# A delta-rule decoder layer: the key scale is made on VectorE in two operations, GpSimd's chains of a head lose two operations, and the order of all instructions is drawn up anew

## The chip, the cores and the metric

The kernel runs on one core of one Trainium2 chip. The time is the device time of one execution in microseconds (us); it is quoted as the median of three runs. The engines are TensorE (PE; its weight loads are shown apart as PEld), VectorE (DVE), ScalarE (ACT), GpSimd (POOL) and SyncE (SP), which here issues the loads and stores. Each engine works through its own instructions strictly in the order in which the program issues them, and waits on semaphores for results of the others.

## The reference

One decoder layer on 2048 tokens of width 1024 in float32: a gated delta-rule mixer with 8 heads of 128, a cross-attention with 4 heads on a memory of 256 rows, an output projection, a layer norm, and a squared-ReLU MLP of width 4096 with a second layer norm. The change lies in the mixer:

```python
qkv = silu(causal_depthwise_conv(qkv, conv_w))
q = l2_normalize(heads(q)); k = l2_normalize(heads(k)); v = heads(v)
beta = sigmoid(b);  g = -exp(a_log) * softplus(a + dt_bias)
# in chunks of 64 tokens, with gc = cumsum(g) and decay = exp(gc_i - gc_j):
lower  = strict_lower((k*beta) @ k.T * decay);   a_mat = I + lower
u      = solve(a_mat, v*beta);  w = solve(a_mat, k*beta*exp(gc))
v_new  = u - w @ state
o      = (q*exp(gc)) @ state + ((q @ k.T) * decay) @ v_new
o      = rms_norm(o, gate_norm_w) * silu(z)
```

`l2_normalize` divides by sqrt(sum of squares + 1e-6). The kernel leaves q and k as they come from the convolution and puts their norms into factors of one number a token. `bh` is such a factor: beta divided by the squared norm of k, which stands on the rows of `lower`.

## The kernel before

**Stages.** The tokens are four blocks of 512. Two blocks form a super. The program runs the mixers of blocks 0 and 1, the output projection of the first super, its first and second MLP product (`ff1`, `ff2`), a stage that prepares the gate `z` of blocks 2 and 3 (`gate_seven`), the mixers of blocks 2 and 3, and the output projection and MLP of the second super. Large products are made of float32 values split into a high and a low half, so that one product is three matmuls of 128x128 on 128x512 (`mm3`; in the profile `aq`, `ak`, `av`, `az` are the projections for q, k, v and the gate, and `fA`, `f2A` and the like belong to the MLP). Weights come by DMA as `wraw` or, split already, as `whl`; `T` is a token tile that was transposed and split, `xj` its raw form at the start.

**A mixer** is a pipeline over its 8 heads. In step t it issues `dense` for head t, `gdn_a` for head t-1 and `gdn_b` for head t-2.

- `dense` makes q, k and v (`aq`, `ak`, `av`, then the convolution in `raw`, `cq`, `ck`, `cv`), transposes k and q on TensorE (`ptk`, `ptq`), and ACT sums their squares into `ss` (four columns for k, four for q; its scratch outputs are `jk`, `jq`). From `ss` GpSimd makes `rk` (power -1/2 of k's part), `e4` (`e` in the profile; from q's part), `vbs`, `bh` and `nbe`.
- `gdn_a` loads a head's decay logarithms (`gb`), makes `dl` and `at` with them, multiplies k with k and q (`pkq`), scales `dl` by `bh` on VectorE, inverts the triangular matrix (`invert`: `inv`, `pp`, `pq`, `Z`, `ZT`, `X`, `Y`), and transposes v (`ptv`), which ACT scales by `vbs`.
- `gdn_b` runs through the chunks with the state (`pc`, `po`); ACT sums the squares of the output into `oss`, GpSimd makes `m4` (`m` in the profile) and `ro` (power -1/2), ACT scales the output (`on`), TensorE transposes it (`pto`) and VectorE multiplies it with the gate.

`gates` makes, once a block, the factors of all heads: `beta`, `betah`, `neg`, the decay sums `gc`.

**What sets the order.** Nothing is issued where it is written. A `Recorder` takes all operations down, and `issue` gives them to the engines in an order that is stored in the program as a table of numbers (`ORDER`); a second table (`SLOT`) says which buffer of its kind each tile gets. Both were made for this list of operations. All recorded instructions therefore have one line in the profile, L615 before and L673 after; groups must be told apart by tile names.

```python
out = [self.ops[i] for i in order()]
...
for o in out:
    o.fn(*[res(a) for a in o.args], **{k: res(v) for k, v in o.kw.items()})
```

Of the kernel before, what the change touches and what calls it, by code (L numbers as in the profile page):

```python
# [14 lines left out]
P = 128  # L15
TB = 512
NC = TB // P
D = 1024
# [153 lines left out]
class Op:  # L172
# [4 lines left out]
    "c-rlK+m7ryuH+A;0qZXP|BsF0LfKiX*6!U8Gr$0iK4-72s!XS?3q=Nl!TZxb>Fa;vbCplke-?gmt@c^{bEO+U<$J%%e5d|8Cx5v1b@rduep%Y*"  # L177
    "!aJ^V^H1ed@TXGwRr{}H?Q87+>_6ah<&!3Uv0voIPw|&{cdq+(a=Ue{JO8-X=YLo4_;0E|e!p<L<Nd4sZJ(O=9kd%S^<Uh7>YuqEbDja&pWAQR"
    "cT#bC`_lWVu6<AY&dR<3o}$e0X}DO$jaG~jK3+0!yZ!ZcfBoP7bX^}`sEz$^FH_g5ciq3iNbhfIpS&<jt#DrUsO|sZZu6dteaHJ!_x$7XIsMa@"
    "UpberH?QB`wx=uafxh<F;tp2V{Pr8aZ=ZVeRy&uBK2p~HOeuBG?7kv~td4sR`ox3mk?o&eu~MdQV?PDHq@1s;{B6O^x5NS37p+=eHG9P--tLuj"  # L180
    "Ke^(5_IKgMzZ?4tUw~<@`$p=(eBWGjTH<vt0o?k``(ZKUcxTxIzjs0z{8oIX@8w%+;q~?#unjPIX|Mjob(gq#_WKJ~(tgN_B~ub-vGjuFv+p0*"
    "%9VQ%tDx*R=C*%V2EI<$ANz^17we~#j<5bNR@xpn4*H%lJx=F7%+rsCUk*%a&HK%G!P{sWslj>OPrX-o|7gSIS-p(*_Q53P#oNE~p6!fbyZ?*("
    "%lfC|rmlf~x9==3OuxRNW6NRs_YCb7MC;<o-wSc>5nM7Y*WL&FUHELCdn@DF@eEwKyvKn#n_(fkmOZDf?U8Qdr$O0^40{qQq{E1815+?JFhP4M"
    "VyrMpSp$Wiw^`Z0ygwuRseGZSEv%ogx%b6z+dcO$!?quwr}A2=xW`UI$ysUp`b8EO6S4;&-dynYnHGERn~}I`GjEE6muSugE%08G`%(9}?JwNB"
    "b?s~JEAMsnwj}$>_8-#T`>FG)^W0GUuQdMZZTiaVX)5Om_J8gb-|zsHyL{jO{{E%QH7=KoJ=gbl?0;ZSVSccCN*y{)_$e&^sr9&$c3kF7U->a^"
    "iP!sjmZ=*}`W-9|J|H{TxDxiy+z^vz*tKoU9?AjpHtxoIyc*8|O!ofnhQ~>Jv3Cw+;v(Q7um==_pZV|;AK`OuL)fr}_WC(52A1~NciLdv+cu=V"
    "$N26gsar4FYI~aaV*O#v*RyQ%`rY1Rt)+Zcb^E0LPg`>6*shq&H8g)%@%yItVYQkp2Y=Xi$=CZP_@HnawhOTh3|DQD3D;V#T;XF6H+IUzD#bHi"
    "_-D26qu{sO%2|h3{$W7I_t_R(2S-RQG%y_-pjTL#vhS_6ire2u()Kd;A;wJ!!v!OeCYD--(b<czby^4PttLC4ZklK8js2U<cf-Vwh3j#}FJ8Fe"
# [443 lines left out]
def hybrid_layer(  # L632
# [46 lines left out]
    def small(name, shape, bufs=3, dt=F32):  # L679
        return rec.buf(sm, shape, dt, name, bufs, name)  # L680
# [1458 lines left out]
```

## Time and profile before

| | |
|---|---|
| runs | 2700.58, 2701.74, 2702.75 us (median 2701.74) |
| the profiled execution's own time | 2704.81 us |
| its span from first to last instruction | 2703.1 us |
| granted TensorE clock, mean | 0.998 of full speed |
| instructions in the profile | 42569 |
| bytes moved by DMA | 633.73 MB, 234 GB/s |

The stages lie in the span at about 0 to 20 us (start), 20 to 345 (mixer of block 0), 345 to 612 (block 1), 612 to 756 (output projection), 756 to 1373 (MLP), 1373 to 1410 (`gate_seven`), 1410 to 1690 (block 2), 1690 to 1965 (block 3), 1965 to 2100 (output projection) and 2100 to 2703 (MLP, last layer norm and store). A row of a group reads: line, engine, operation, output<-inputs, shapes, count, then busy us and mean ns of one, then the idle time of the engine just ahead of such instructions and what ended it. A row of waits reads: engine, what it was about to run, what it waited for, then us in total, how many, the longest.

### The profile page before, as it was taken

Reading aid. Unit: us, or ns where it says so; the run is one execution under the profiler, and the core shown is the slowest. Engines: PE = TensorE matmul, PEld = TensorE weight load, DVE = VectorE, ACT = ScalarE, POOL = GpSimd, SP = SyncE. Lnnn points to the kernel's source line nnn. Section 1 sums busy time; section 2 is a strip of 40 time slices with the busy share of each in tenths; the row PEclk is TensorE's granted clock in tenths of the full one; section 3 lists DMA queues with packets and bytes.
Section 4 is the critical chain, followed back from the end, with each engine's and each line's share of the span. In section 5 each row is a group of like instructions: output and inputs, shape, how many; then the busy total and the mean of one; then the engine's idle time right before and its main releaser. Section 6 shows DMA issues by size and latency. Waiting matters only on the chain.

```text
span 2703.1 us, 42569 instructions
## 1 busy us (share of the span) xinstructions
PE 2681.2 (99%) x13553; PEld 2248.4 (83%) x13553; DVE 2129.6 (79%) x5658; ACT 1643.1 (61%) x4128; POOL 426.5 (16%) x1023
## 2 busy tenths in 40 slices
PE   9999999999999999999999999999999999999998
PEld 7888888888888888878888888888888888888887
DVE  7999889998877776766787887999978656567475
ACT  7778767786575555333445777777756555544342
POOL 3233233331000000000012332332201000000011
PEclk9999999999999999999999999999999999999999
DMA  8767558877888888889785444545678654486673
GB/s 296 262 216 280 185 181 288 310 255 264 279 296 299 298 294 287 293 273 297 239 289 206 150 140 157 182 154 181 211 263 285 216 177 147 153 288 218 209 236 123
DMA packets 222896, 633.73 MB, mean 234 GB/s; under 512 B 25648, under 2 KB 34256, under 8 KB 203728
## 3 DMA queue, kind: packets, MB, share of 16 engines
q1 hardware_dynamic: 222240, 630.97, 67.8%
q8 instruction: 107, 1.75, 0.3%
q14 instruction: 117, 0.96, 0.1%
q10 hardware_dynamic: 432, 0.05, 0.0%
HBM read 446.83 MB, written 184.09 MB: 233 GB/s over the span
## 4 chain that ended last, share of the span: by engine, by line
PE 92%; DVE 5%; DMA 1%; ACT 1%; issue 1%; POOL 0%; POOLq 0%; ACTq 0%; DVEq 0%; SPq 0%
PE fA L615 13%; PE f2A L615 13%; PE ao L615 8%; PE f2C L615 6%; PE fC L615 6%; PE az L615 6%; PE av L615 6%; PE aq L615 6%; PE ak L615 5%; PE f2B L615 3%; PE fB L615 3%; PE pc L615 3%; PE amq L615 3%; PE po L615 2%; PE pkq L615 1%; PE pq L615 1%
## 5 line engine op out<-in xcount | busy, mean ns | idle before, releaser
L615 ACT CAST whl<-wraw 128x512 fp32r<-128x512 f32 (+2 forms) x294 | 226.0, 779 | 193.4 <-PE fC L615 58.9
L615 DVE TENSOR_TENSOR whl<-wraw,whl 128x512 fp32r<-128x512 f32 (+2 forms) x294 | 257.5, 885 | 92.6 <-ACT whl L615 88.2
L615 PE MATMUL fA<-B,whl 128*128 128x512 f32 x1152 | 291.4, 389 | 0.0
L615 PE MATMUL f2A<-whl,X 128*128 128x512 f32 x1152 | 266.0, 390 | 0.0
L615 PEld LDWEIGHTS f2A<-whl,X 128*128 128x128 f32 x1152 | 217.2, 189 | 45.2
L615 PEld LDWEIGHTS fA<-B,whl 128*128 128x128 f32 x1152 | 216.3, 188 | 44.9
L615 ACT CAST X<-X 128x1024 fp32r<-128x1024 f32 x118 | 123.2, 1050 | 177.4 <-DMA X<-xsc 132.5
L615 PE MATMUL av<-T,whl 128*128 128x512 f32 x768 | 224.6, 405 | 0.6 <-DMA whl<-wsc 0.6
L615 PE MATMUL aq<-T,whl 128*128 128x512 f32 x768 | 218.5, 404 | 2.7 <-ACT T L615 1.3
L615 PE MATMUL ak<-T,whl 128*128 128x512 f32 x768 | 220.0, 403 | 0.0
L615 DVE TENSOR_TENSOR X<-X,X 128x1024 fp32r<-128x1024 f32 x118 | 143.4, 1221 | 83.6 <-ACT X L615 83.3
L615 PE MATMUL fC<-B,whl 128*128 128x512 f32 x768 | 199.3, 389 | 0.0
L615 PE MATMUL az<-T,whl 128*128 128x512 f32 x624 | 182.1, 405 | 0.0
L615 PE MATMUL f2C<-whl,X 128*128 128x512 f32 x768 | 177.4, 390 | 2.3 <-ACT X L615 2.3
L615 POOL TENSOR_SCALAR ve<-mv 128x1 f32<-128x1 f32 x34 | 20.5, 603 | 987.2 <-DVE mv L615 984.8
L615 PEld LDWEIGHTS f2C<-whl,X 128*128 128x128 f32 x768 | 144.3, 188 | 32.7 <-ACT X L615 2.7
L615 PEld LDWEIGHTS fC<-B,whl 128*128 128x128 f32 x768 | 144.2, 188 | 29.9
L615 ACT CAST whl<-whl 128x1024 fp32r<-128x1024 f32 x92 | 96.7, 1053 | 114.3 <-DMA whl<-tsc 80.7
L615 PEld LDWEIGHTS aq<-T,whl 128*128 128x128 f32 x768 | 139.1, 190 | 29.5 <-ACT T L615 1.8
L615 PEld LDWEIGHTS ak<-T,whl 128*128 128x128 f32 x768 | 138.0, 189 | 23.0
L615 PEld LDWEIGHTS av<-T,whl 128*128 128x128 f32 x768 | 137.1, 189 | 22.4 <-issue 1.0
L615 DVE TENSOR_TENSOR whl<-whl 128x1024 fp32r<-128x1024 f32 x92 | 112.0, 1220 | 45.9 <-ACT whl L615 45.6
(305 smaller groups left out, 6439.8 us busy)
## 6 DMA issues: line engine op xcount, KB each, us to landing
whl<-wsc SPq DMA_DIRECT2D x100, 1024.0 KB, 5.3
wraw<-in_w_ff_dram SPq DMA_DIRECT2D x106, 512.0 KB, 5.0
X<-xsc SPq DMA_DIRECT2D x96, 512.0 KB, 4.5
wsc<-whl SPq DMA_DIRECT2D x36, 1024.0 KB, 6.3
whl<-tsc SPq DMA_DIRECT2D x64, 512.0 KB, 4.7
xsc<-hB SPq DMA_DIRECT2D x96, 256.0 KB, 3.5
xo<-cat SPq DMA_DIRECT2D x80, 256.0 KB, 5.5
wraw<-in_w_in_dram SPq DMA_DIRECT2D x35, 512.0 KB, 4.4
```

Of the source, the lines that this page charges most:

```text
L615: o.fn(*[res(a) for a in o.args], **{k: res(v) for k, v in o.kw.items()})
```

## The change

**In `gates`**, `1 + exp(-b)`, which is 1/beta, is kept as `ib` in two buffers; `beta` becomes a temporary from which only `betah` is made. The number of operations stays.

**In `dense`**, `bh` is made on VectorE as the reciprocal of (`ss` + 4 eps) times `ib`, from k's part of `ss` alone; before, it was beta times `rk` twice, on GpSimd, after an add over both parts. The add on GpSimd now covers k's four columns and writes `rk`; q's add goes into the operation that makes `e4`. The two parts of `ss` are told apart for the dependencies (`.part(0)`, `.part(1)`), so what needs k's part no longer waits for q's.

**In `sumsq`** the squares are taken of the output times 128^-1/2, and the scaling ahead of `m4` goes.

```diff
-        nc.vector.tensor_scalar_add(eb, eb, 1.0)
-        G["beta"] = small("beta", sh, 2)
-        nc.vector.reciprocal(G["beta"], eb)
+        ib = G["ib"] = small("ib", sh, 2)
+        nc.vector.tensor_scalar_add(ib, eb, 1.0)
+        beta = small("beta", sh, 1)
+        nc.vector.reciprocal(beta, ib)
...
-                                     accum_out=ss[:, n * NC + c:n * NC + c + 1])
+                                     accum_out=ss[:, n * NC + c:n * NC + c + 1].part(n))
...
-        nc.gpsimd.tensor_scalar_add(ss, ss, 4 * RMS_EPS)
+        bh = res["bh"] = small("bh", [P, NC])
+        nc.vector.scalar_tensor_tensor(out=bh, in0=ss[:, :NC].part(0), scalar=4 * RMS_EPS, in1=G["ib"][:, h], op0=ALU.add, op1=ALU.mult)
+        nc.vector.reciprocal(bh, bh)
         rk = small("rk", [P, NC])
-        nc.gpsimd.tensor_tensor(out=rk, in0=ss[:, :NC], in1=mhalf, op=ALU.pow)
-        res["e4"] = small("e4", [P, NC], 4)
-        nc.gpsimd.tensor_scalar_mul(res["e4"], ss[:, NC:], P * RMS_EPS)
+        nc.gpsimd.tensor_scalar_add(rk, ss[:, :NC].part(0), 4 * RMS_EPS)
+        nc.gpsimd.tensor_tensor(out=rk, in0=rk, in1=mhalf, op=ALU.pow)
...
-        bh = res["bh"] = small("bh", [P, NC])
-        nc.gpsimd.tensor_tensor(out=bh, in0=G["beta"][:, h], in1=rk, op=ALU.mult)
-        nc.gpsimd.tensor_tensor(out=bh, in0=bh, in1=rk, op=ALU.mult)
+        res["e4"] = small("e4", [P, NC], 4)
+        nc.gpsimd.tensor_scalar(out=res["e4"], in0=ss[:, NC:].part(1), scalar1=4 * RMS_EPS, scalar2=P * RMS_EPS, op0=ALU.add, op1=ALU.mult)
...
-            nc.scalar.activation(j, p3[:, c], AF.Square, accum_out=o[:, c:c + 1])
+            nc.scalar.activation(j, p3[:, c], AF.Square, scale=P ** -0.5, accum_out=o[:, c:c + 1])
...
-        nc.gpsimd.tensor_scalar_mul(m4, oss, 1.0 / P)
-        nc.gpsimd.tensor_tensor(out=m4, in0=m4, in1=e4, op=ALU.add)
+        nc.gpsimd.tensor_tensor(out=m4, in0=oss, in1=e4, op=ALU.add)
```

**`ORDER` and `SLOT`** are replaced as a whole. The start of one slot table, as an example:

```diff
     ("sp", "iv"): (
-        "13203012012331021203031230120312"
+        "13022130312023103102302120313021"
```

What stands where is seen in the rows of the engines' programs. In each pair below the rows of before come first; `x2` counts equal rows in a row, and numbers behind a name tell buffers apart.

SP at the program's start (loads of raw token tiles, of the first weights, and of small parameters):

```order
L615 DMA xj<-in_xt_dram 128x512
L615 DMA wraw<-in_w_in_dram 128x256
L615 DMA wraw<-in_w_in_dram 128x512
L615 DMA xj<-in_xt_dram 128x512 x2
L615 DMA wraw<-in_w_in_dram 128x256
L615 DMA lnr<-in_mem_ln_b_dram 8x128
```

```order
L673 DMA wraw<-in_w_in_dram 128x256 x2
L673 DMA xj<-in_xt_dram 128x512
L673 DMA alog<-in_a_log_dram 128x8
L673 DMA xj<-in_xt_dram 128x512 x3
L673 DMA wraw<-in_w_in_dram 128x512
```

The first token tile went out first, and now goes out behind two pieces of weights; the second of these stood behind three token tiles.

PE in the first product for q (each k-slice of the input takes three `aq` matmuls; `aab` makes the gates' inputs and reads all eight raw token tiles):

```order
L615 MATMUL aq<-T_170,whl 128x512
L615 MATMUL aq<-T_180,whl 128x512
L615 MATMUL aq<-T_170,whl 128x512 x2
L615 MATMUL aq<-T_180,whl 128x512
L615 MATMUL aq<-T_170,whl 128x512
L615 MATMUL pln<-ident,lnr 128x32
L615 MATMUL aab<-xj,abw 32x512 x8
```

```order
L673 MATMUL aq<-T_172,whl 128x512
L673 MATMUL aq<-T_182,whl 128x512
L673 MATMUL aq<-T_172,whl 128x512
L673 MATMUL warm<-ones 128x128
L673 MATMUL aab<-xj,abw 32x512 x8
L673 MATMUL aq<-T_172,whl 128x512
L673 MATMUL aq<-T_182,whl 128x512
L673 MATMUL aq<-T_172,whl 128x512
```

The `aab` matmuls stood behind six k-slices and now stand behind five.

PE in block 1, from the end of the inversion (`pp`) to the transposes of v (`ptv`) of its first head:

```order
L615 MATMUL pp<-inv 128x64 x2
L615 MATMUL az<-T_4285,whl 128x512
L615 MATMUL az<-T_4287,whl 128x512
L615 MATMUL az<-T_4285,whl 128x512 x2
L615 MATMUL ak<-T_4285,whl 128x512
L615 MATMUL ak<-T_4287,whl 128x512
L615 MATMUL pc<-state,ck 128x128
L615 MATMUL ptv<-ident,cv 128x128 x4
```

```order
L673 MATMUL pp<-inv 128x64 x2
L673 MATMUL az<-T_4267,whl 128x512
L673 MATMUL az<-T_4252,whl 128x512 x2
L673 MATMUL ak<-T_4252,whl 128x512
L673 MATMUL ptv<-ident,cv 128x128 x4
```

Six projection matmuls and a `pc` stood between the two; now it is four projection matmuls.

POOL about the end of the same head's chunks (`m`, `ro`):

```order
L615 TENSOR_TENSOR nbe<-bh,neg 128x4
L615 AFFINE_SELECT at<-gb 128x512
L615 COPY inv<-dl 32x2x32
L615 COPY inv<-Z_5990 32x2x32
L615 TENSOR_SCALAR m_6134<-oss 128x4
L615 TENSOR_TENSOR m_6134<-m_6134,e_5521 128x4
L615 TENSOR_TENSOR ro<-m_6134,mhalf 128x4
```

```order
L673 AFFINE_SELECT dl<-gb 128x512
L673 TENSOR_TENSOR rk<-rk,mhalf 128x4
L673 COPY inv<-dl 32x2x32
L673 TENSOR_TENSOR m_6159<-oss,e_5113 128x4
L673 TENSOR_TENSOR ro<-m_6159,mhalf 128x4
L673 TENSOR_TENSOR vbs<-betah,rk 128x4
```

The scaling of `oss` is gone, and a power for `rk` and a `vbs` now stand near the pair that remains.

DVE in the same place (the gates of the next block are being made):

```order
L615 COPY gc<-pg 128x32
L615 TENSOR_TENSOR gc<-pg,gc 128x32
L615 TENSOR_SCALAR gc<-gc 128x32
L615 SCALAR_TENSOR_TENSOR ck<-raw,cw,ck 128x512
L615 COPY gct<-pgt 32x128
```

```order
L673 COPY gc<-pg 128x32
L673 SCALAR_TENSOR_TENSOR ck<-raw,cw,ck 128x512 x2
L673 TENSOR_TENSOR gc<-pg,gc 128x32
L673 SCALAR_TENSOR_TENSOR bh<-ss,ib 128x4
L673 TENSOR_SCALAR gc<-gc 128x32
L673 RECIPROCAL bh<-bh 128x4
L673 COPY gct<-pgt 32x128
```

The two new operations stand in VectorE's order between those of the gates, with one other between them.

Over the whole program GpSimd has 96 instructions fewer and VectorE 64 more. TensorE's matmuls are the same in number and shape and stand in another order; changes from one product's kind to another's (the wide ones and the small float32 ones) go from 1277 to 1227.

More of the change, by code (lines that the diff above doesn't have):

```diff
@@ new lines @@
+    "-d{+(h~KRJs+G^T^v~Mw%*8)rznki3_We%z%)0;SpE*87KibzZ_Lb}p_P1946kXf?%KmG8>VDA{zaIJ--|PFYUiN4E!`k+X(LZB+YTuVryUw*Q"
+    "s_0V6eyi)azA^vroA#+He`H;E_b}|M|IYU5L!a#b_Nh1b?M~lPDp_atF{bW(-;Pe1KV#qj{_&%~_w|*vFRUzG*!Yae^|fbzT66J>{>h2)+dpg1"
+    "{*jMbHHu~JFXiqRRnLK!x(se1*ZtppkZ;|iJIbduePJ-@Rihe%%P6Fz3mZD)zWkb|4yij#I<>|=7mc+(*k9GiFffzhNPF1y%c`$Tu4H_;j{VjB"
+    "-K>XS_D$)<eV3V4&RA=d(tc8T#4z`zd!GBK8n41o<it}ddqV8H&t>|@Wnc3i`pn4guXF1kUAcZ-bctn8m!essIawDsuQ{7_<NB~JU4SNV-cL8r"
+    "IMJSb8qu=PuNSFlWa_>c-KJiY{YPdl?g45%>wU<jaorc69-VKG=%aDp*T;qJ37a_T@TA*=p@VZ4t){(@re?q%vC8z*+k5hBcIr5F?pxHN(|L6Y"
@@ L482 @@
+    "Uqq+^8_@ch9a{&nSPM&Rz990c?x=Hj7^h+|EwfNq>K1u`_op(uz49Ya%JtD5;?dphRBt)5j9P37G4)8}6!F{u@d!F?WOE6~CwpI>KNv}jeudV#"
+    "t@MNi3Cv5RGeZ~Wi1*H@H&o)C+H&M2X^uIxzPPI&sq_9la~|Pr@pZVo{oX6q>EObT|NRB53++V"
 )
@@ L503 @@
-        "213021302130213021302130213"
+        "0123102310231231201302310312023012031231023212301312020313202130312302013210123203121303210301230121"
+        "0312030121032103203120312301230123102130213021302130321032103210321032103210321032103210321023102310"
+        "2310231021303210321032013201023120130213213021031203213203102130213021301203123102302331023101323021"
+        "3120321021301232010321032103231203120312031203120312031203120312031203120312031203120312031203120312"
+        "031203120312031203120320132"
@@ L509 @@
+        "64637160277014217015474706413505224607351467324602150210521052105210521052105210527143605"
     ),
     ("ps", "acc"): (
[L511 to L513 removed]
+        "1021021021021202012012012220221201012100021021012201012102021021021012201001212012102121021021201201"
@@ L983, in gates @@
         nc.vector.tensor_scalar_mul(G["neg"], eg, -1.0)
-        nc.vector.tensor_scalar_add(eb, eb, 1.0)
-        G["beta"] = small("beta", sh, 2)
-        nc.vector.reciprocal(G["beta"], eb)
+        ib = G["ib"] = small("ib", sh, 2)
+        nc.vector.tensor_scalar_add(ib, eb, 1.0)
+        beta = small("beta", sh, 1)
+        nc.vector.reciprocal(beta, ib)
         G["betah"] = small("betah", sh, 2)
-        nc.vector.tensor_scalar_mul(G["betah"], G["beta"], 0.5)
+        nc.vector.tensor_scalar_mul(G["betah"], beta, 0.5)
         pt = bank("pgt", "m")
```

715 lines of the change are left out of this document (380 added, 335 removed).

## The prediction

> **What bounds the kernel now.** I read the page's shares first, then the time by stage, then TensorE's waits.
>
> The page's first part and its chain (columns: busy us, share, instructions; shares of the span):
> ```profile
> PE 2681.2 (99%) x13553; PEld 2248.4 (83%) x13553; DVE 2129.6 (79%) x5658; ACT 1643.1 (61%) x4128; POOL 426.5 (16%) x1023
> PE 92%; DVE 5%; DMA 1%; ACT 1%; issue 1%; POOL 0%; POOLq 0%; ACTq 0%; DVEq 0%; SPq 0%
> ```
> TensorE (PE) is idle for 2703.1 - 2681.2 = 21.9 us. The time by stage says where (window, its length, busy us of PE, PEld, DVE, ACT, POOL with counts, granted clock, DMA share, GB/s): the start, the four token mixers (blocks 0 to 3), a pure first-MLP stage, and the last stage.
> ```profile
> 0.00:20.00 20.00, 16.08 (x68) 10.50 (x69) 9.78 (x20) 10.09 (x18) 3.58 (x17) 0.91 0.80 243
> 20.00:345.00 325.00, 324.83 (x1850) 277.18 (x1850) 295.70 (x1039) 256.00 (x772) 97.19 (x236) 1.00 0.68 246
> 345.00:612.00 267.00, 263.85 (x1522) 225.72 (x1520) 247.18 (x979) 202.42 (x699) 94.51 (x225) 1.00 0.75 261
> 1410.00:1690.00 280.00, 279.14 (x1588) 237.88 (x1588) 234.07 (x920) 200.28 (x677) 82.06 (x223) 1.00 0.48 169
> 1690.00:1965.00 275.00, 273.37 (x1620) 235.22 (x1619) 251.54 (x1028) 209.06 (x729) 84.41 (x214) 1.00 0.52 180
> 2100.00:2390.00 290.00, 290.00 (x1281) 240.18 (x1280) 182.47 (x279) 164.29 (x283) 0.00 (x0) 1.00 0.51 175
> 2390.00:2703.00 313.00, 304.98 (x1346) 252.29 (x1344) 199.57 (x235) 113.11 (x117) 14.55 (x16) 0.99 0.63 214
> ```
> Idle PE is 3.9 us at the start, 8.0 us in the last stage (the last layer norm and store, whose instructions stand as before), and about 10 us in between. The changed arithmetic lives in the mixers alone, where PE already works 98.8 to 99.9% of the time. PE's waits in between (us in total, times, longest):
> ```profile
> PE f2C L615 <- ACT X L615: 2.3, 1, 2.3
> PE pto L615 <- ACT on L615: 1.8, 1, 1.8
> PE ptv L615 <- ACT Y L615: 1.6, 4, 0.5
> PE pt L615 <- ACT st L615: 1.4, 1, 1.4
> PE av L615 <- DMA whl<-wsc: 0.6, 1, 0.6
> ```
> These five are 7.7 of the 10 us. So a change that leaves PE's work alone can gain at most about 10 us in the middle and a little at the start. 0.2% of the time, about what a measurement of this kernel can tell from no change, is 5.4 us.
>
> **GpSimd's shorter chains.** The operations concerned (busy us, mean ns | idle before):
> ```profile
> L615 POOL TENSOR_SCALAR ss<-ss 128x8 f32<-128x8 f32 x32 | 12.5, 391 | 241.9 <-ACT jq L615 232.3 <-DVE cv L615 9.5
> L615 POOL TENSOR_SCALAR e<-ss 128x4 f32<-128x4 f32 x32 | 9.9, 310 | 2.6
> L615 POOL TENSOR_TENSOR bh<-bh,rk 128x4 f32<-128x4 f32 x32 | 9.4, 294 | 1.8
> L615 POOL TENSOR_TENSOR bh<-beta,rk 128x4 f32<-128x4 f32 x32 | 8.9, 278 | 1.9
> L615 POOL TENSOR_SCALAR m<-oss 128x4 f32<-128x4 f32 x32 | 9.1, 285 | 177.5 <-ACT joss L615 177.4
> L615 DVE SCALAR_TENSOR_TENSOR dl<-pkq,bh,dl 128x128 f32<-128x128 f32 x128 | 42.2, 344 | 3.6 <-PE pkq L615 2.9 <-ACT dl L615 0.3
> ```
> Both bh multiplies and the 1/P scaling of oss go: 9.4 + 8.9 + 9.1 = 27.4 us. The add on ss narrows from 8 to 4 columns (12.5 to about 9.9, by the e row), 2.6 us more. So GpSimd loses 30 us of 426 and 96 instructions. It is busy 16% and carries 0% of the chain, so this by itself is 0. The ACT square takes the factor 1/P as its scale at no new instruction. bh now needs neither q's squares nor the power: the old chain ran, in one head of block 3,
> ```profile
> 1923.42 0.61 POOL L615 TENSOR_SCALAR ss<-ss 128x8 f32<-128x8 f32 x1 [10.34 <-ACT jq L615]
> 1924.12 1.04 POOL L615 TENSOR_TENSOR rk<-ss,mhalf 128x4 f32<-128x4 f32 x1
> 1925.51 0.20 POOL L615 TENSOR_TENSOR bh<-bh,rk 128x4 f32<-128x4 f32 x1
> 1927.16 0.34 DVE L615 SCALAR_TENSOR_TENSOR dl<-pkq,bh,dl 128x128 f32<-128x128 f32 x1
> ```
> that is 1925.71 - 1923.42 = 2.3 us from add to bh, then 1.4 us of slack until its reader dl. The dl group's idle time names PE and ACT and never GpSimd: bh was in time. The earlier bh buys slack where none was missing, so 0.
>
> One GpSimd chain did stop PE, the 1.8 us at pto (start us, us):
> ```profile
> 440.10 0.27 POOL L615 TENSOR_SCALAR m<-oss 128x4 f32<-128x4 f32 x1 [2.27 <-ACT joss L615]
> 440.45 3.07 POOL L615 TENSOR_TENSOR m<-m,e 128x4 f32<-128x4 f32 x1
> 443.60 1.04 POOL L615 TENSOR_TENSOR ro<-m,mhalf 128x4 f32<-128x4 f32 x1
> 443.84 0.74 DVE L615 SCALAR_TENSOR_TENSOR cq<-raw,cw,cq 128x512 f32<-128x512 f32 x1
> 446.13 0.66 PE L615 MATMUL pto<-ident,on 128*128 128x128 f32 x4 [1.78 <-ACT on L615]
> ```
> An add that is a fraction of a microsecond elsewhere was held for 3.07. The scaling ahead of it goes (0.35 us), the held kind of add stays, and what runs beside it is redrawn. Between losing the whole 1.8 and nothing I take half: -0.9 us.
>
> The Trainium skill (SBUF — State Buffer, Who interferes with whom) says that a VectorE instruction with two SBUF inputs and a GpSimd one that reads SBUF exclude each other, the later one waiting whole. The 3.07 us add agrees with that. By the rule the new add-multiply (ss and ib, both SBUF) could also be held behind the power that now starts beside it, which is a rival priced below from rows; the row at 443.84 speaks against it.
>
> **VectorE's two new operations.** Nearest rows:
> ```profile
> L615 DVE SCALAR_TENSOR_TENSOR nb<-mv,rs 128x1 f32<-128x1 f32 x18 | 2.7, 153 | 5.0 <-POOL rs L615 4.9
> L615 DVE SCALAR_TENSOR_TENSOR gp<-gp,gz 128x32 f32<-128x32 f32 x28 | 5.4, 193 | 0.4
> L615 DVE RECIPROCAL rc<-su 128x2 f32<-128x2 f32 x32 | 5.1, 158 | 0.7 <-ACT pr L615 0.4
> L615 DVE RECIPROCAL beta<-geb 128x32 f32<-128x32 f32 x4 | 1.4, 344 | 0.0
> ```
> With 4 columns I stay near the narrow ends: 160 + 165 ns a head, 32 heads, 10.4 us (bounds 10.0 and 17.2). Idle VectorE time in the four mixers is 29.3, 19.8, 45.9 and 23.5 us, so 2.6 us each is covered; in block 1 cover falls to 17.2. VectorE has 5% of the chain, so I charge 5%: +0.5 us (bounds 0 and 2). The gate edits (ib kept, beta now a temporary) keep the number of instructions: 0.
>
> **The redrawn order.** Most of the price is here, since every engine's rows move.
>
> (a) Groups of small matmuls. Each group inserted among the 512-wide ones costs PE a little beyond its work:
> ```profile
> 1431.60 0.60 PE L615 MATMUL ptq<-ident,cq 128*128 128x128 f32 x4
> 1431.95 2.56 PE L615 MATMUL aq<-T,whl 128*128 128x512 f32 x10
> 1434.36 0.40 PE L615 MATMUL pkq<-kq 128*128 128x256 f32 x2
> ```
> In the pure stage a 512-wide matmul comes every 290.0 / 1281 = 0.226 us. Here ten of them take 2.41 us and four transposes ahead of them 0.35, 2.76 in all. Ten at 0.226 are 2.26, four transposes at about 0.11 (pto: 0.66 us for four with a tail of some 0.2) 0.44, together 2.70. So a group costs about 0.05 us. Counted over PE's rows, changes between the wide fp32r and the small fp32 kind fall from 1277 to 1227, 25 groups less: -1.3 us (bounds -2 and 0).
>
> (b) ptv after pp. In the head whose rows stand with the change above (block 1's first), four wide matmuls now stand between pp and ptv where six (and a pc) stood; over all heads, those with four or fewer wide ones' worth go from 9 to 16 of 32. The 1.6 us of ptv waits, plus shorter ones, grow: +1.0 us (bounds 0 and +2).
>
> (c) The start. SP issued the first token tile first; now two weight pieces go ahead of it, and all aab matmuls stand ahead of the sixth k-slice, so they wait for the last token tile.
> ```profile
> 0.79 0.39 SPq L615 DMA_DIRECT2D xj<-in_xt_dram  x1
> 8.45 0.33 SPq L615 DMA_DIRECT2D xj<-in_xt_dram  x1
> 13.00:15.00 2.00, 2.00 (x6) 1.46 (x5) 1.80 (x4) 0.63 (x2) 0.00 (x0) 0.50 0.64 204
> 15.57 1.92 PE L615 MATMUL aab<-xj,abw 128*32 128x512 f32 x16
> ```
> The first product starts some 0.9 us later, but the next weight load moves two places forward (an issue takes 0.33 to 0.39 us and a little between, so 0.5 to 1 us earlier), and a pause before aab can cost time at the granted clock of 0.50 that the row shows. -0.5 us (bounds -2 and +1.5).
>
> (d) Loads. Counted as matmul work between the PE instruction that releases a load's issue and the first that reads it, 14 loads had under 8 us, now 9. The 0.6 us wait of av: -0.3 (bounds -0.6 and 0). At the 2.3 us f2C wait the second-MLP rows of SP stand in the same sequence: 0 (bounds -2.3 and +1). The pt wait: 0 (bounds -1.4 and +1.4).
>
> **Sum.** -0.9 + 0.5 - 1.3 + 1.0 - 0.5 - 0.3 = -1.5 us. Against the profiled execution (span 2703.1, its own time 2704.81) that gives 2703.3. That execution stands 3.1 us above the median of the runs, 2701.74, so I carry the difference to the median: 2700.2 us. Not all ends come together: the low ends add to -10.1 (-1.8 - 2 - 2 - 0.6 - 2.3 - 1.4), the high ends to +7.9 (2 + 2 + 1.5 + 1 + 1.4); four fifths of them are -8.1 and +6.3, which from 2701.7 gives 2693.6 to 2708.0.
>
> **Rivals.**
> 1. Clearly faster: the new order clears the five waits (7.7 us) and (a) holds (1.3). 2692.7 us. For it: all are accidents of order, and bh now comes earlier. Against: three of the five lie where the change puts nothing, and new rows make new accidents. Chance 0.17.
> 2. Slower, VectorE held at bh. The add-multiply sits in VectorE's strict order and waits for ACT's last k square, or behind GpSimd's power (1.04 us); behind it queue dl and the inversion that PE's pq needs. GpSimd stood 232.3 / 29 = 8.0 us a head waiting for the q squares, so such waits are not small. It decides once the hold eats block 1's idle VectorE time: 19.8 / 8 = 2.5 us a head less 0.3, that is 2.2. At 3 us a head, (3.3 x 8) - 19.8 = 6.6 us in block 1 and 2.9 in block 3: 2711 us. Against: at 443.84 a two-input operation ran at its usual 0.74 beside a power. Chance 0.08.
> 3. Slower by a new long stall at the start or in the load queue, with a stretch at half clock like the one after 13.00 us: two more stalls the size of f2C's with some 2 us of slow clock each, 8 us: 2708 to 2710. Chance 0.07.
> 4. The forecast, within 0.2%: 0.68. It includes the case that the shorter chain moves nothing at all and only order accidents show.
>
> Faster by over 0.2%: rival 1 and a little of the forecast's low end, 0.18. Slower: rivals 2 and 3, 0.15. Same: 0.67. The range 2693.6 to 2708.0 leaves out most of rival 2 and parts of 1 and 3.
>
> **What the profile after would show.** Right: GpSimd near 396 us and 927 instructions, VectorE near 2140 and 5722; PE busy near 2680; bh on VectorE at about 160 ns each; no VectorE wait for ACT's jk of more than a microsecond or two at bh; PE waits in the middle of 8 to 11 us, ptv's above 2. Wrong: a VectorE row for bh with tens of us of idle time ahead of it; a PE wait of over 2 us that has no counterpart now; a start whose first 20 us hold under 15 or over 17.5 us of PE work.

## The result: 5.5 us slower, and where the time went by the profile after

The changed kernel takes 2706.55 us (median of 22 runs) against 2701.07 of the kernel before (22 runs): a ratio of 1.0021, interval 1.0014 to 1.0027. One of before's 22 runs, in a slow state, took 2949.53 us, and the ratio leaves it out. The forecast was 2700.2, so the sign is wrong, though the time lies inside the forecast's range (2693.6 to 2708.0), near its upper end. The profiled execution of before stood 3.7 us above what its median became with more runs. Every ratio below, with its 95% interval, is to runs of before that were taken along with the kernel in question.

The page of the kernel after (busy us, share, instructions; shares of the chain):

```profile
PE 2688.4 (99%) x13553; PEld 2245.3 (83%) x13553; DVE 2147.6 (79%) x5722; ACT 1642.4 (61%) x4128; POOL 388.6 (14%) x927
PE 92%; DVE 4%; ACT 1%; DMA 1%; issue 1%; POOL 0%; POOLq 0%; DVEq 0%; SPq 0%; ACTq 0%
```

GpSimd lost its 96 instructions and 38 us. TensorE's busy time rose by 7.2 us with the same 13553 records, and its idle time fell, from 21.9 to 18.0 us. The longer time is therefore *inside* what the page calls busy. By stage (the same windows as before):

```profile
0.00:20.00 20.00, 15.95 (x61) 10.83 (x62) 7.99 (x16) 9.52 (x17) 2.52 (x14) 0.83 0.82 269
345.00:612.00 267.00, 265.17 (x1525) 224.91 (x1525) 251.70 (x994) 200.03 (x698) 89.15 (x202) 1.00 0.76 264
1410.00:1690.00 280.00, 279.21 (x1580) 235.78 (x1579) 239.51 (x930) 199.41 (x672) 73.10 (x203) 1.00 0.49 171
1690.00:1965.00 275.00, 273.04 (x1604) 232.58 (x1603) 254.55 (x1035) 208.68 (x725) 72.38 (x188) 1.00 0.50 176
```

The counts tell more than the busy times here: in 1690 to 1965 TensorE got through 1604 matmuls where it had done 1620, and in 1410 to 1690 through 1580 where it had done 1588, while "busy" over 99% of the time in both. (In 345 to 612 it did 1525 for 1522; there the kernel before had its 1.8 us wait.) Its waits, groups of interest:

```profile
PE aq L673 <- ACT T L673: 2.6, 2, 1.9
PE ptv L673 <- ACT Y L673: 1.4, 4, 0.5
PE pp L673 <- ACT inv L673: 0.8, 3, 0.4
PE pq L673 <- DVE Xc L673: 0.5, 1, 0.5
PE pkq L673 <- DVE Bc L673: 0.5, 1, 0.5
PE pto L673 <- ACT on L673: 0.2, 1, 0.2
```

Of the waits of before, the 1.8 us at pto has shrunk to 0.2, and the 1.4 at pt, the 2.3 at f2C and the 0.6 at av are gone. `bh` on VectorE is as priced (operation, count, duration in ns as least, median, most, then first and last start; the last row is a wait):

```profile
L673 DVE SCALAR_TENSOR_TENSOR bh<-ss,ib x32: 123/156/260, 48.0 to 1926.3; 128x4 f32<-128x4 f32 x32
L673 DVE RECIPROCAL bh<-bh x32: 157/170/178, 48.8 to 1927.9; 128x4 f32<-128x4 f32 x32
  ACT jk L673: 0.7, 1
```

VectorE sat idle for ACT's squares once, 0.7 us, in front of these. The longest add-multiply took 0.26 us, so none was held for a power of 1.04 us; in this trace five of the 32 ran while GpSimd was in the middle of a power, and took 0.15 to 0.20 us. By the rule of the Trainium skill (SBUF — State Buffer, Who interferes with whom) they could have been held; no run here shows it. The move made a wait on the other side, GpSimd's for `bh` ahead of `nbe`: 21.8 us in four waits here and 21.2 in nine with the same arithmetic in the old order, so it does not set the two apart.

### The profile page after: what moved, and what is told of

It reads as the page before. It is cut to its first block, busy times and chain, and to the rows that moved or that the text cites. A ratio compares the mean times of both kernels' runs of the same rounds, so it can differ in the third digit from the quotient of the medians.

```text
span 2706.4 us, 42498 instructions
## 1 busy us (share of the span) xinstructions
PE 2688.4 (99%) x13553; PEld 2245.3 (83%) x13553; DVE 2147.6 (79%) x5722; ACT 1642.4 (61%) x4128; POOL 388.6 (14%) x927
## 4 chain that ended last, share of the span: by engine, by line
PE 92%; DVE 4%; ACT 1%; DMA 1%; issue 1%; POOL 0%; POOLq 0%; DVEq 0%; SPq 0%; ACTq 0%
PE fA L673 13%; PE f2A L673 12%; PE ao L673 9%; PE f2C L673 6%; PE fC L673 6%; PE av L673 6%; PE aq L673 6%; PE az L673 6%; PE ak L673 5%; PE fB L673 3%; PE f2B L673 3%; PE amq L673 3%; PE pc L673 3%; PE po L673 2%; PE pkq L673 2%; PE pq L673 1%
```

## Experiments 1: arithmetic or order

The order is bound to the list of operations, and the two lists differ in a few places only, so the arithmetic of one kernel could be issued in the order of the other. The first kernel is the changed one with before's `ORDER` and `SLOT`, where the two `bh` operations take the places of the two multiplies:

```diff
-POOL TENSOR_TENSOR bh<-beta,rk
-POOL TENSOR_TENSOR bh<-bh,rk
+DVE SCALAR_TENSOR_TENSOR bh<-ss,ib
+DVE RECIPROCAL bh<-bh
```

> The changed kernel's arithmetic (bh on VectorE, the shorter GpSimd chains) issued in the order and the slots of the kernel before: the two new VectorE operations stand where GpSimd's two bh multiplies stood. It differs from the kernel after in order and slots alone, and from the kernel before in the arithmetic alone. Theory 1, the order costs the time (a later start and small matmuls set nearer to what they wait for): within 2 us of before, and 4 to 7 us faster than after. Theory 2, the arithmetic costs it (VectorE's 64 new operations, 17.7 us more VectorE work): 4 to 7 us slower than before, like after.

Measured: 2697.95 us, ratio to before 0.9987 (0.9978 to 0.9996). The new arithmetic in the old order is *faster* than before, by 1 to 6 us, and beats both kernels. Against it the kernel after, which differs in order and slots alone, is 0.0034 slower (plus or minus 0.0011 with both intervals): 9 us, of 6 to 12. In the trace TensorE's and ScalarE's rows are those of before, one for one. The second kernel is before with one part of the change:

```diff
-            nc.scalar.activation(j, p3[:, c], AF.Square, accum_out=o[:, c:c + 1])
+            nc.scalar.activation(j, p3[:, c], AF.Square, scale=P ** -0.5, accum_out=o[:, c:c + 1])
...
-        nc.gpsimd.tensor_scalar_mul(m4, oss, 1.0 / P)
-        nc.gpsimd.tensor_tensor(out=m4, in0=m4, in1=e4, op=ALU.add)
+        nc.gpsimd.tensor_tensor(out=m4, in0=oss, in1=e4, op=ALU.add)
```

> The kernel before, order and slots too, with one part of the change alone: the factor 1/128 goes into the squares on ScalarE and GpSimd's scaling of oss goes; bh stays on GpSimd. The new arithmetic in the old order was 3.6 us faster than before (ratio 0.9987 to one run's before; the 1.8 us hold at pto was gone from its trace). If the shorter chain to ro is what gained: 1.5 to 4 us faster than before, and no hold at pto over 0.5 us. If bh on VectorE gained: within 1 us of before, the hold still there.

Measured: ratio 0.9998 (0.9989 to 1.0007); one hold of 0.2 us was left at pto. So the long hold was gone with the scaling alone (one execution), and the time did not show it: neither of the two expectations came true whole. Which part of the arithmetic gains the 0.0013 isn't separated by these intervals.

The new arithmetic in the old order, its page and the windows of blocks 1 to 3:

```profile
PE 2680.3 (99%) x13553; PEld 2247.0 (83%) x13553; DVE 2132.9 (79%) x5722; ACT 1641.1 (61%) x4128; POOL 400.8 (15%) x927
345.00:612.00 267.00, 265.97 (x1536) 227.35 (x1535) 249.47 (x1003) 203.32 (x704) 85.77 (x202) 1.00 0.76 263
1410.00:1690.00 280.00, 279.77 (x1602) 238.81 (x1601) 238.88 (x958) 201.27 (x682) 75.23 (x203) 1.00 0.48 167
1690.00:1965.00 275.00, 273.92 (x1616) 235.67 (x1615) 252.63 (x1042) 210.46 (x739) 78.37 (x191) 1.00 0.51 179
```

In the same stretches 11, 22 and 12 matmuls more than after (not quite the same work, as after is some us late when each begins). The busy sum is 8.1 us lower (2680.3 against 2688.4), the idle time 16.9 against 18.0.

## Experiments 2: where in the program, and the start

Marks of progress are the first or last start of a tile's matmuls (the two numbers behind the durations): the first `f2A<-whl,X` ends the first super's first MLP product, the last `fA<-B` the second super's. New arithmetic in the old order, then after:

```profile
L610 PE MATMUL f2A<-whl,X x1152: 388/389/398, 1056.9 to 2601.9; 128*128 128x512 f32 x192
L610 PE MATMUL f2A<-whl,xl x128: 388/389/478, 1315.8 to 2688.7; 128*128 128x512 f32 x128
L610 PE MATMUL fA<-B,whl x1152: 387/389/398, 774.8 to 2384.1; 128*128 128x512 f32 x192
```

```profile
L673 PE MATMUL f2A<-whl,X x1152: 387/389/497, 1063.3 to 2611.1; 128*128 128x512 f32 x192
L673 PE MATMUL f2A<-whl,xl x128: 388/389/475, 1321.3 to 2697.8; 128*128 128x512 f32 x128
L673 PE MATMUL fA<-B,whl x1152: 387/389/496, 780.0 to 2393.1; 128*128 128x512 f32 x192
```

After is 6.4 us late at 1063, 5.5 at 1321, 9.0 at 2393, and 9.1 at the last matmul: the loss lies in both halves ahead of the MLPs' ends, none in the last 300 us. (2.3 us of it stand at the start of this one execution of after; see below.)

Four kernels try places. The old start: the first 184 operations in before's order, the rest in after's.

> The kernel after with the first 184 operations (to about 25 us, TensorE's first 90 matmuls) in the order of before, the rest in the order of after. Theory 1 (start plus near matmuls): the first product starts at about 5.5 us again and not at 7.3, and 1 to 2.5 us are gained on after; still 3 to 4.5 us slower than before. Theory 3, the start is all of it (late tiles and slow clock that never is caught up): as fast as before, 5 us gained.

The old first half and the new first half, cut at the first matmul of the first MLP product:

> The arithmetic of after; order of before up to the first first-MLP matmul (start, blocks 0 and 1, output projection, to about 750 us), order of after from there. In the two traces the kernel after lags by 5.0 us when the second MLP product of the first super starts, and gains 3.6 of it back at one wait of before (f2C) that may be that execution's alone; blocks 2 and 3 add 3.0. Theory 1: 4 to 6 us faster than after, 0 to 3 slower than before. If blocks 2 and 3 make the difference: 2 to 4 us faster than after.

> The arithmetic of after; order of after up to the first first-MLP matmul, order of before from there, slots given out anew. If the order's cost sits in the second half (the run with the old first half gained nothing): within 2 us of the new arithmetic in the old order (2698 us). If both halves cost: 2701 to 2704 us. If the first half has it all: 2705 to 2708 us.

For these three the slots had to be given out anew (the buffer that came free first), so the same was done to the order of after, as a control:

> A control: order and arithmetic of after, with slots given out anew, always the one that came free first in the order (about 130 of some 2600 tiles get another predecessor in their buffer). If only the order counts: within 2 us of after. If waits for buffers matter: 2 to 5 us slower, and then the runs with the old start, the wide matmuls pulled ahead, and the old first half, which had such slots too, are to be compared with this one.

```diff
-order = new;                          slots = new
+order = old[:184] + rest of new;      slots = by age   (old start)
+order = old[:cut] + rest of new;      slots = by age   (old first half)
+order = new[:cut] + rest of old;      slots = by age   (new first half)
+order = new;                          slots = by age   (control)
```

Measured: control 1.0028 (1.0017 to 1.0039), old start 1.0030 (1.0020 to 1.0041), old first half 1.0025 (1.0016 to 1.0034), new first half 1.0034 (1.0022 to 1.0047). The control differs from after in its slots alone and is 1.9 us slower, plus or minus 3.5, so new slots cost nothing that is clear of noise. (The old slots were not tried with the new order; what is called the order's cost below holds that remainder.) The old start gains nothing on the control, though its first product started at 5.4 us and the control's at 6.9: at the gates' transposes both were level.

```profile
L667 PE MATMUL pgt<-ident,gc x4: 271/272/293, 46.8 to 1697.6; 128*96 128x128 f32 x4
L665 PE MATMUL pgt<-ident,gc x4: 271/275/293, 46.9 to 1698.6; 128*96 128x128 f32 x4
L673 PE MATMUL pgt<-ident,gc x4: 271/278/293, 49.3 to 1699.6; 128*96 128x128 f32 x4
```

(control, old start, after). The profiled execution of after itself reached this mark at 49.3 us, with a granted clock of 0.83 in its first 20 us; the new arithmetic in the old order was there at 47.0. The other kernels with the new start reached it between 46.0 and 47.4, and those with the old start between 46.4 and 48.1, so the 2.3 us are taken as that execution's own and not as the price of the start's order. The two half-and-half kernels were no faster than after, outside every case that was expected of them. Old first half, then new first half:

```profile
L645 PE MATMUL f2A<-whl,X x1152: 388/389/500, 1057.5 to 2609.0; 128*128 128x512 f32 x192
L645 PE MATMUL f2A<-whl,xl x128: 388/389/475, 1315.6 to 2695.6; 128*128 128x512 f32 x128
L633 PE MATMUL f2A<-whl,X x1152: 388/389/397, 1061.4 to 2613.2; 128*128 128x512 f32 x192
L633 PE MATMUL f2A<-whl,xl x128: 387/389/504, 1321.1 to 2700.1; 128*128 128x512 f32 x128
```

With the old first half the kernel is level with the old order at 1057 and 1316 and loses 6.9 by the end (2695.6 against 2688.7). With the new one it is 4.5 late at 1061; then holds of 2.1, 1.8 and 2.3 us at `f2A`, `f2C` and `pmo`, where the unedited old order had 1.1 at `f2C` and nothing over 0.2 at the other two, eat what the old second half gives. So each half of the new order loses 4 to 7 us by the marks, and the halves can't be added up. These holds stand at 1360, 1195 and 1984 us, far behind the cut at about 750 us, and this kernel's slots are new too; what caused them is not shown.

## Experiments 3: what kind of loss

The two groups of TensorE whose busy time rose most, and the group of small matmuls that rose most (busy us, mean ns), old order with new arithmetic, then after:

```profile
L610 PE MATMUL aq<-T,whl 128*128 128x512 f32 x768 | 218.1, 404 | 2.1 <-ACT whl L610 0.9 <-DVE T L610 0.5 <-ACT T L610 0.4
L610 PE MATMUL az<-T,whl 128*128 128x512 f32 x624 | 182.0, 404 | 0.0
L610 PE MATMUL pc<-state,ck 128*128 128x128 f32 x240 | 47.2, 278 | 0.0
```

```profile
L673 PE MATMUL aq<-T,whl 128*128 128x512 f32 x768 | 220.9, 405 | 2.9 <-ACT T L673 2.6 <-DVE T L673 0.2
L673 PE MATMUL az<-T,whl 128*128 128x512 f32 x624 | 184.5, 403 | 0.0
L673 PE MATMUL pc<-state,ck 128*128 128x128 f32 x240 | 48.5, 284 | 0.1
```

A wide matmul is shown with 0.389 us from start to end but one starts every 0.226. If the next one is held for less than the difference, 0.16 us, the hold counts as the wide one's busy time, and the list of waits doesn't have it. To find such holds, take the time from each matmul's start to the next one's. Compare it with like places, where the matmul and its two neighbours are of the same three kinds, in five traces (the three below and the two kernels with room on VectorE further down), and call usual the time that only a tenth of the like places undercut. What exceeds the usual by 0.04 to 0.7 us is counted as a short hold, from 20 us on and without `aab` (2.9 us in every kernel):

| | short holds | us in all | of it inside busy time | usual times, sum |
|---|---|---|---|---|
| new arithmetic, old order | 84 | 11.5 | 8.2 | 2629.6 |
| after | 163 | 20.4 | 15.2 | 2631.4 (11 matmuls more) |
| control | 174 | 21.6 | 16.1 | 2628.8 (2 matmuls fewer) |

That is the loss: the short holds grow by 9 us, 7 of them inside the busy time. The usual times agree within about 1 us once the matmuls more or fewer are allowed for (some 0.2 us each), so a rival is out: the new order does not pay more for changes between kinds of matmul. The lag of 9.1 us between the two executions is nearly accounted for: 2.3 at the start and 8.9 of short holds, less 2.2 of holds above 0.7 us that went, make 9.0. The growth is at small matmuls: pq from 1.4 to 3.9 us, pc from 1.6 to 3.8, pp from 1.6 to 3.6, ptv from 3.0 to 3.8. Block 0 adds 0.7 us, block 1 2.0, block 2 2.6 and block 3 2.5. Before itself has 12.7 us of short holds. Where after's list of waits has a row for one of these, what it waited for came from VectorE or ScalarE.

Three explanations were tried. **Near producers.** Counted in matmul work, 108 small matmuls stand under 0.7 us behind the matmul that they depend on through another engine in the old order, 161 in the new. First cure them: 164 wide matmuls of after put ahead of small ones that were held.

```diff
 MATMUL pc<-state,ck 128x128
 MATMUL pq<-ZT_1587,inv 128x32
+MATMUL ak<-T_172,whl 128x512
 MATMUL po<-vt,at 128x128
...
 MATMUL pc<-vt,kd 128x128
-MATMUL ak<-T_172,whl 128x512
 MATMUL pp<-inv 112x32 x2
```

> The kernel after, where 164 times a wide projection matmul that stood behind a small matmul that TensorE was held at (over 60 ns by the trace of after, 18.4 us of holds in all) stands ahead of it; nothing else moves. Theory 1, small matmuls that stand too near to their producers cost the time: half to most of the 18.4 us would be gained where the hold is a wait that 0.227 us of other work covers; allowing for chains that get longer, 5 to 12 us faster than after, so as fast as before or faster. Rival 4, these holds are a fixed cost of changing between the kinds of matmul, or only move down the chain: within 2 us of after.

Measured: 1.0051 (1.0038 to 1.0063), some 8 us slower than after. (Its slots were given out anew, and pairs of small matmuls are split.) The edit did not cure the holds: all short ones together rose from 20.4 to 26.8 us, those at pc from 3.8 to 5.1 and at ptk from 0.4 to 1.6, while those at pq and pp hardly fell (3.9 to 3.7, 3.6 to 3.3). That the chains became longer and were late elsewhere is a guess. Then the reverse, in the old order: 83 small matmuls put one wide matmul nearer, and 83 far ones as a control.

```diff
 MATMUL aq<-T_4291,whl 128x512
-MATMUL aq<-T_4289,whl 128x512
 MATMUL pc<-R,Y 128x128
-MATMUL aq<-T_4289,whl 128x512
+MATMUL aq<-T_4289,whl 128x512 x2
```

> The new arithmetic in the order and slots of before; in blocks 1 to 3, 83 small matmuls (pc 49, pp 26, po 8) that stand 0.7 to 1.1 us of matmul work behind the matmul that they depend on through VectorE or ScalarE are put ahead of the wide matmul before them, 0.227 us nearer. Small matmuls under 0.7 us go from 108 to 146 (161 in the order of after). Theory 1, nearness costs: in the traces the holds are 25 to 45 ns longer for near ones, and up to 0.2 us where the chain really takes as long, so 3 to 7 us slower than 2698. If nearness does not matter: within 1.5 us of 2698, like the control.

> The control: the same swap for 83 small matmuls (pq 34, po 31, pc 15, pp 3) that stand over 2.2 us behind what they depend on. Theory 1: within 1.5 us of 2698. Theory 6, any edit of an order that was fitted as a whole costs 4 to 6 us: 2702 to 2704 us.

Measured: nearer 1.0000 (0.9991 to 1.0008), control 0.9997 (0.9988 to 1.0006). Both stand 0.001 above the unedited 0.9987, and not apart from each other (0.8 us, plus or minus 3.4). Nearness of single matmuls is not shown to be the cause; a cost of up to some 4 us is not excluded by these intervals.

**VectorE's overlap.** VectorE got 14.7 us busier by the order alone (2132.9 to 2147.6). A reason is in its records (after, start and us):

```profile
401.58 0.16 DVE L673 TENSOR_TENSOR Bc<-Bc,Lc 128x4 f32<-128x4 f32 x1
401.67 0.68 DVE L673 TENSOR_TENSOR kq<-cq,kq 128x512 fp32r<-128x512 f32 x1
...
404.93 0.17 DVE L673 STREAM_SHUFFLE Bc<-Xc 128x16 f32<-128x16 f32 x1
405.13 0.18 DVE L673 TENSOR_TENSOR Bc<-Bc,Lc 128x16 f32<-128x16 f32 x1
```

The unrelated operation starts 0.07 us ahead of the other's end, the one that reads its neighbour 0.03 after it. Over all adjacent pairs of the trace the medians are 0.08 ahead and 0.035 behind. The old order has 752 adjacent dependent pairs on VectorE, the new 946, nearly all in the inversion's chain of `Xc` and `Bc`. Spread them (178 operations of after pulled in between, above the dots), then pack the old order's chain to the same 946 (below); TensorE's rows stay as they are:

```diff
 STREAM_SHUFFLE Bc<-Xc 128x20
-TENSOR_TENSOR Bc<-Bc,Lc 128x20
 SCALAR_TENSOR_TENSOR ck<-raw,cw,ck 128x512
+TENSOR_TENSOR Bc<-Bc,Lc 128x20
...
 TENSOR_TENSOR Bc<-Bc,Lc 128x4
-TENSOR_TENSOR at<-pkq,at 128x256
 TENSOR_TENSOR Xc<-Xc,Bc 128x4
+TENSOR_TENSOR at<-pkq,at 128x256
```

> The kernel after with its own slots; on VectorE alone 178 operations that stood up to four places behind an adjacent pair of the inversion's chain (Xc, Bc; the second reads the first) are put between the pair, so that pairs of adjacent operations of which the second reads the first go from 946 to 755 (before's order with the same arithmetic has 752). In the traces a VectorE operation that reads the one ahead of it starts 0.035 us after that one's end, one that doesn't starts 0.08 us ahead of its end. Theory 5, the new order lost that overlap: 191 pairs x 0.115 = 22 us of VectorE time in mixers where VectorE is over 90% busy come back, and 4 to 8 us of the time. Theory 1, it is TensorE's small matmuls that stand too near: within 2 us of after. If the moved operations make the chain itself late: up to 10 us slower than after.

> The mirror of that: the new arithmetic in the order and slots of before, with 237 VectorE operations that stood between two operations of the inversion's chain put behind the second, so that adjacent dependent pairs go from 752 to 946, as in after. TensorE's order is untouched. Theory 5: 4 to 8 us slower than the same kernel without this edit (2698 us). Theory 1: within 2 us of that. If the inversion's chain, now sooner done, is what TensorE waits for: 1 to 4 us faster.

Measured: spread 1.0040 (1.0027 to 1.0052), some 5 us *slower* than after, with VectorE 11.6 us less busy:

```profile
PE 2689.2 (99%) x13553; PEld 2244.3 (83%) x13553; DVE 2136.0 (79%) x5722; ACT 1641.1 (61%) x4128; POOL 385.6 (14%) x927
```

So the overlap came back and the time did not. That does not clear the overlap, as the same edit sets operations of the inversion's chain later, the case that the expectation also allowed for: the short holds rose from 20.4 to 24.4 us, at pc from 3.8 to 6.6. Packed: 1.0010 (1.0001 to 1.0019), 6 us slower than the unedited 0.9987, as theory 5 said; here the short holds rose from 11.5 to 15.6 us with TensorE's own order untouched. To tell lost overlap from late operations, each half of the packing and a spread with narrow operations alone were run; their edits are of the same two forms.

> As the run with the packed chain (new arithmetic, order and slots of before), but only convolution, split and gate operations (cq, ck, cv, kq, cz, whl and the like), 158 of them, go from between two operations of the inversion's chain to behind the second; R, state, dl, at and the inversion's own copies stay. Adjacent dependent pairs go from 752 to 888. Theory 5a, VectorE's lost overlap is what costs (136 of the 194 pairs): 3 to 5 us slower than 2698. Theory 5b, it costs because R, state, dl and inv, for which TensorE waits, come later: within 1.5 us of 2698.

> The other half: only operations that TensorE's small matmuls or the chains wait for (inv, cat, state, R, dl, at and the like), 153 of them, go behind the second; adjacent dependent pairs go from 752 to 868. Theory 5a: 2.5 to 4.5 us slower than 2698. Theory 5b: 4 to 7 us slower, as much as the packed chain's whole edit.

> The kernel after with its own slots; as the run with the spread chain, but only 84 narrow operations (inv, bh, state, R, at, rc and the like, 0.15 to 0.4 us each) are pulled between adjacent pairs of the chain, no 512-wide one. Adjacent dependent pairs go from 946 to 857. Theory 5 (a or b): 89 x 0.115 = 10 us of VectorE time back and the waited-for operations sooner: 2 to 5 us faster than after. Theory 6, any edit by hand of this order sets something else late, as the two spreading edits so far did: 0 to 5 us slower than after.

Measured: 1.0013 (1.0004 to 1.0022), 1.0011 (1.0002 to 1.0020) and 1.0035 (1.0022 to 1.0048). The two halves of the packing cost 7.0 and 6.5 us against 6.2 for the whole, each plus or minus 3.4, and the narrow spread gains nothing on after (3.8 us slower, plus or minus 3.9). No dose is seen; costs in proportion to the pairs (4.3 and 3.7 us) still lie inside the intervals. That convolutions put later cost nothing is excluded; that any such edit costs does not separate the other theories.

**A queue without room.** Take work off one engine and move nothing. One pair of kernels leaves out half of each convolution step (VectorE), the other the tanh (ScalarE; VectorE multiplies by c in its place), in both orders.

```diff
-nc.vector.scalar_tensor_tensor(out=c, in0=raw[:, j:j + TB], ...
+nc.vector.scalar_tensor_tensor(out=c[:, :TB // 2], in0=raw[:, j:j + TB // 2], ...
...
-nc.scalar.activation(th, c, AF.Tanh, scale=0.5)
```

> The kernel after, order and slots too, with the three convolution steps of each of the 96 projections (VectorE, 128x512, about 0.74 us each) done on the first 256 columns alone, so about 0.37 us each and some 107 us less VectorE work in the mixers; the convolution of the other half is left out. To be read against the same edit in the old order. Theory 5, VectorE's queue makes the new order slower: the gap of 9 us between the two orders shrinks to under 4. Theory 1, TensorE's own places (or ScalarE): it stays at 7 to 11.

> The same edit (half the convolution left out) with the new arithmetic in the order and slots of before. TensorE waits little there: 0 to 8 us faster than without the edit (2698 us).

> The kernel after, order and slots too, without the 96 tanh operations of the convolutions (ScalarE, 128x512, 0.63 us each, 60 us in all); VectorE multiplies c by itself in place of the tanh, so that half of the activation is left out. To be read against the same edit in the old order. If ScalarE's queue, or the chain from projection to transposes that is now shorter, makes the new order slower: the gap of 9 us shrinks to under 4. If VectorE's queue or TensorE's own places: it stays at 6 to 11.

> The same edit (tanh left out) with the new arithmetic in the order and slots of before: 0 to 6 us faster than without the edit (2698 us).

| | old order | new order | gap |
|---|---|---|---|
| as it is | 0.9987 (0.9978 to 0.9996) | 1.0021 (1.0014 to 1.0027) | 0.0034 |
| room on VectorE | 0.9969 (0.9958 to 0.9980) | 0.9996 (0.9987 to 1.0005) | 0.0027 |
| room on ScalarE | 0.9993 (0.9984 to 1.0001) | 1.0024 (1.0014 to 1.0034) | 0.0031 |

```profile
PE 2675.3 (100%) x13553; PEld 2248.6 (84%) x13553; DVE 2063.0 (77%) x5722; ACT 1639.4 (61%) x4128; POOL 374.0 (14%) x927
PE 2681.7 (99%) x13553; PEld 2245.7 (83%) x13553; DVE 2076.2 (77%) x5722; ACT 1640.7 (61%) x4128; POOL 362.6 (13%) x927
```

(room on VectorE, old order, then new). Room on VectorE gains some 5 to 7 us in either order, so VectorE's queue does cost time, but about the same in both: the gap stays at 7 us, its interval some 4 us to each side. The short holds fall to 5.0 us in the old order and 14.1 in the new (44 and 126 of them), and are still 9 us apart. Room on ScalarE gains nothing and leaves 8, plus or minus 3.5. Neither queue is seen to be the cause of the gap by itself.

## Why the prediction was wrong, point by point

**The step that failed** is the pricing of the redrawn order, parts (a) to (d), put at -1.1 us in all, and above all (b). It took the list of waits for all of TensorE's waiting and priced, beside a saving by the count of groups, one edge of it, ptv, at +1.0. The list leaves out holds shorter than the tail of the matmul ahead: 8.2 us in the old order with the new arithmetic, 15.2 in after; all short holds together rise by 9 us, and the new order costs 6 to 12. "PE busy near 2680" was named among the signs of being right; it came to 2688.4. Waits in the middle of 8 to 11 us were another; from 20 us to the last matmul TensorE's idle time was 5.7 us, where before had 9.9. None of the three signs of being wrong came: the forecast had no sign for a loss inside busy time.

- (a) Fewer changes between the kinds of matmul, -1.3: not seen. The usual times of all matmuls, which hold the price of such changes, agree within about 1 us, and busy time rose by 7 to 8 us with 25 groups fewer.
- (b) ptv +1.0: measured in the waits -0.2 (1.6 to 1.4). The mechanism, small matmuls waiting for chains through other engines, was right in kind and sat at pq, pc and pp as well, which were not priced: +9 of short holds where +1 stood, of which ptv has 0.8.
- (c) The start, -0.5: no gain and no loss is seen. The first product started 1.8 us later, not 0.9; by 47 us the control was level with the old start, and the 2.3 us that after's own execution was late there are its own.
- (d) The 0.6 us at av went (-0.3 was set), but by luck: it is gone in the old order with the new arithmetic too, so the load order need not have done it. The 2.3 us at f2C, left at 0, went as well. With TensorE's rows in the same order it was 1.1 with the new arithmetic, 0.7 without the scaling and absent with the chain packed, one execution each; what sets its size is open, and it may be part of why the profile of before stood high.
- The arithmetic: 38 us of GpSimd work went where 30 were forecast (the other 8 are not accounted for); `bh` took 156 and 170 ns where 160 and 165 were set. VectorE's +0.5 was no loss that shows: the arithmetic alone, put at -0.4 with the pto term, is 1 to 6 us faster, and which part of it gains is open. The sum took the order for a term of about its size, and it is the larger one.
- pto, -0.9: 1.6 of the 1.8 went in the trace, and with the scaling alone too; in the time it is lost among runs that differ by several us.
- Rival 1 (five waits cleared, 2692.7): four of the five waits did go, and the time rose. Rival 2 (held at bh): one wait of 0.7 us, and none of the five that ran beside a power was held; excluded. Rival 3 (a new stall with slow clock) has a time near the measured one but not the mechanism: no new wait over 1.9 us; that one, at the start, came with a slow clock (0.83 over 20 us) in after's execution, and the old start changed nothing.

**What stays open.** That the order (with its slots) costs 6 to 12 us, mostly in the blocks from 1 on, in short holds at small matmuls, is shown. The start and the arithmetic are excluded as its cause; slots given out anew, and room on VectorE or on ScalarE, do not change it by more than their intervals of some 4 us, and room on GpSimd was not tried. What property of the order makes the holds is not settled: single distances and VectorE's overlap are neither confirmed nor excluded, as edits by hand cost some 2 to 8 us whichever way they went, most with intervals of 3 to 4 us to each side. One engine's whole order was not exchanged for the other's.

## What to carry to other kernels

Where an engine is 99% busy, ask what the busy time holds: compare the number of its instructions in equal stretches, and the distance from each to the next with that of its like elsewhere, before calling what the list of waits shows all there is to win or lose. When a change brings new arithmetic and a new order, price and test them apart; here the arithmetic in the old order (2697.95 us) was the better kernel, and the new order hid it. One execution can be late by itself, as after's start was: a mark from several kernels tells. An order that was fitted as a whole is no sum of local choices: of eleven kernels that altered an order in part, none was faster than the order that it started from.

## What the runs showed of the hardware

On VectorE an operation that doesn't read its neighbour's result starts 0.08 us ahead of that one's end, one that does 0.035 us after it (medians over the adjacent pairs in the trace of after); the two differ by 0.115 us. Spreading 191 dependent pairs took 11.6 us off VectorE's busy time, some 0.06 us a pair, and nothing off the kernel's.

In these profiles a 128x512 matmul is shown with 0.389 us and the next starts 0.226 us after it, so a hold of under 0.16 us behind one is not in the list of waits. 8.2 and 15.2 us of short holds were inside busy time in the two orders, with TensorE 99% busy in both.
